# Residual sums of the down projection: VectorE, or ScalarE copies with adding transfers

## The chip, the cores and the metric

The kernel runs on one core of one Trainium2 chip. A core has five engines, each with its own queue of instructions that it works off in order: TensorE (PE in the profile, its weight loads PEld), VectorE (DVE), ScalarE (ACT), GpSimd (POOL) and SyncE (SP). They meet only through semaphores: an instruction that waits holds up everything behind it on its engine. Transfers between the memories run on 16 DMA engines shared by all queues; here SyncE issues the plain loads and GpSimd the adding transfers (`accum_op=ALU.add`), which add what they bring to what the destination holds. Matrix products accumulate in PSUM, whose banks hold 128 x 512 numbers each, and must be read out of it before a bank is used again. All else that is computed on lies in the on-chip memory SBUF.

The metric is the time of one execution in microseconds (us), less is better. Before the change: median 821.08 us of 3 runs (821.05 to 822.15).

## The reference

One decoder layer on 512 tokens of 1024 channels in float32. A mixer (convolution branch, gated linear attention branch, merge, output projection `w_o`) comes first; then the channel mixer, in which the change lies:

```python
h = h + merged @ w_o[l]

u2 = _rmsnorm(h, norm2_g[l])
z = _causal_dwconv(u2 @ w_ffn_up[l], ffn_dw_w[l], ffn_dw_b[l])
h = h + (jax.nn.silu(z[..., :FFN_DIM]) * z[..., FFN_DIM:]) @ w_ffn_down[l]
return _rmsnorm(h, final_g)
```

FFN_DIM is 2816, that is 22 blocks of 128 channels. What concerns us is the last sum: `h` plus the down projection.

## The kernel before

**Products.** Every product in float32 is made of three: each operand is split into a high part rounded to a shorter format (`hi`, cast by ScalarE, L355 or L385) and the rest (`lo`, a subtraction by VectorE, L356 or L390), and `mm3` (L444) multiplies lo by hi, hi by lo and hi by hi into one bank (L448 to L450).

**The residual.** `hres[t, n]` are eight tiles of 128 tokens by 512 channels (t = 0 to 3, n = 0, 1) that hold `h` from the output projection to the end.

**The down projection in three groups.** The 22 channel blocks go in pairs, and the pairs in three groups (`GROUPS`): four pairs, three pairs, four pairs. In each group the up projection of its pairs is computed (`up_plan`), partly together with the first pair of the next group, and then `seven("w_down", ...)` multiplies the group's pairs with `w_ffn_down`. It does so by Strassen's scheme: seven products of block sums in place of eight. The steps have names, in this order: a11; a12 and s1, each in two halves that alternate; n2, s4, n3, a22. Each step makes two products (i = 0 and 1, one for each tile of 128 tokens of one half). Each of the two goes to a bank of its own: a11, n2, n3 and a22 to the pair of banks "x", s1 and s4 to the pair "y", a12 to the pair "z". a11, a12 and s1 start their banks afresh, the others go on adding to what is in theirs. After each product the bank is added to, or subtracted from, one `hres` tile: 14 sums a group (L1419, in `add`), all by VectorE. In the first group a product of one step and one i takes 12 matrix instructions, in the second, with three pairs, 9.

So a bank has to be read before the next step writes it: n3 fills the x banks, its two results are read, and a22 goes on adding to the same banks directly after. Which tiles a step's results go to is written in `into`: a11 and a12 go to `hres[0, 0]` and `hres[1, 0]`; n2 and s4 to `hres[0, 1]` and `hres[1, 1]`; s1 and n3 to `hres[2, 1]` and `hres[3, 1]`; a22 to `hres[2, 0]` and `hres[3, 0]`.

**Weights.** They come in tiles of 128 x 1024 (512 KB; 256 KB where half a tile is needed) into four `raw` buffers or two `kept` buffers, loaded by SyncE (L253, L257, L296). For the scheme, sums of blocks of the weight are needed, too. Three kinds of instruction on GpSimd make them: L300, an adding transfer that sums n3's weight, one for each half; L317, an adding transfer onto `kept`, twice in each group for each half, the second time for a22's weight; and, in the up projection, L327, four additions of 128 x 512 for every pair of tiles (`two_sums`): three after the split of x1's weight and one after the split of x3's. x1, x3, x2 and x4 are the four parts of such a pair's products; x3's weight is what the first two L327 make.

**What sets the order.** Each engine's instructions are put into their order by a planner when the kernel is built; some lines tie it down. In `seven`, the weights that are prepared at a22's call are to be issued behind the last sum of n3 (`freed`). Weights are split two ahead of their use (`LOOK`).

**Small buffers.** `tmp()` gives one of six buffers of 128 x 512 in turn. Until now they serve the up projection: the convolution over tokens (L1500, L1503, L1511) and the pair products (L1181, L1184).

## Time and profile before

| | |
|---|---|
| median of 3 runs | 821.08 us |
| the profiled execution | 820.78 us |
| its span, first to last instruction | 818.9 us |
| TensorE, busy | 810.3 us (99%) |
| VectorE, busy | 715.6 us (87%) |
| ScalarE, busy | 448.9 us (55%) |
| GpSimd, busy | 148.8 us (18%) |
| granted clock of TensorE, mean | 0.999 |
| VectorE's residual sums of 128 x 512, mean of one | 671 ns |

The profile is that of one execution, taken by the hardware profiler. A group line of the page reads: line of the kernel, engine, operation, result <- operands, sizes, count | busy us in total, mean ns of one | idle time of the engine ahead of them, and what ended most of it. A timeline row reads: start, length in us, engine, line, operation; the bracket at the end is the idle time before it and what ended that. A row of a table by stretches gives for each stretch the busy time and count of PE, PEld, DVE, ACT and POOL, then the granted clock, the DMA engines' mean busy share, and GB/s. A row of DMA issues ends with the median time from issue to landing. Times in the timeline run from the span's start; the first group's down projection runs from about 570 to 608 us, the second's from about 671 to 700.

### The profile page before, as it was taken

How to read it: one execution, taken by the hardware profiler on the slowest of the kernel's cores; microseconds unless marked ns; L12 is line 12 of the kernel's file. 1: busy time of each engine (PE TensorE's matmuls, PEld its weight loads, DVE VectorE, ACT ScalarE, POOL GpSimd, SP SyncE). 2: the span in 40 equal slices, each digit the busy share in tenths (PEclk: the TensorE clock that was granted, in tenths of full speed). 3: DMA queues.
4: the chain of work that ended last, by engine and by line, in shares of the span. 5: the costliest groups of instructions: out<-in, count | busy, mean ns of one | idle time of the engine just before them, and what ended most of it. 6: DMA issues, size and time to landing. Idle time of an engine off the chain costs nothing.

```text
span 818.9 us, 11480 instructions
## 1 busy us (share of the span) xinstructions
PE 810.3 (99%) x4287; PEld 700.5 (86%) x4287; DVE 715.6 (87%) x1157; ACT 448.9 (55%) x666; POOL 148.8 (18%) x133
## 2 busy tenths in 40 slices
PE   9999999999999999999999999999999999999996
PEld 7888888888888889999988898898889988899885
DVE  6689999999989699885788889979965999789896
ACT  6643447656663446684444556556435663466554
POOL 2000010001000213633001000230123301622012
PEclk9999999999999999999999999999999999999999
DMA  8355572563532123223657623146642447334662
GB/s 318 104 127 144 148 188 96 130 154 104 120 97 96 49 62 109 88 78 129 206 115 220 187 71 103 52 161 166 134 137 89 144 123 167 104 103 177 158 129 102
DMA packets 30615, 106.25 MB, mean 130 GB/s; under 512 B 3464, under 2 KB 3600, under 8 KB 30560
## 3 DMA queue, kind: packets, MB, share of 16 engines
q1 hardware_dynamic: 24784, 85.34, 30.4%
q0 software_dynamic: 5760, 20.19, 14.4%
q8 instruction: 33, 0.54, 0.3%
q14 instruction: 22, 0.18, 0.1%
q10 hardware_dynamic: 16, 0.00, 0.0%
HBM read 103.42 MB, written 2.10 MB: 129 GB/s over the span
## 4 chain that ended last, share of the span: by engine, by line
PE 98%; DMA 1%; ACT 0%; DVE 0%; POOL 0%; issue 0%; POOLq 0%; SPq 0%; ACTq 0%
PE mm L448 28%; PE mm L449 28%; PE mm L450 28%; PE mm L662 3%; PE ax L450 2%; PE ax L448 2%; PE ax L449 2%; PE ax L1070 1%; PE ax L1072 1%; PE ax L1051 1%; DMA raw<-in_w_v_dram 1%; PE ax L1040 0%; PE ax L529 0%; PE ax L576 0%; PE ax L1085 0%; PE mm L933 0%
## 5 line engine op out<-in xcount | busy, mean ns | idle before, releaser
L448 PE MATMUL mm<-uh,wlo 128*128 128x512 f32 (+1 forms) x672 | 244.4, 364 | 0.0
L449 PE MATMUL mm<-ul,whi 128*128 128x512 f32 (+1 forms) x672 | 242.4, 361 | 0.0
L450 PE MATMUL mm<-uh,whi 128*128 128x512 f32 (+1 forms) x672 | 242.0, 360 | 0.0
L450 PEld LDWEIGHTS mm<-uh,whi 128*128 128x128 f32 x672 | 126.8, 189 | 19.4
L448 PEld LDWEIGHTS mm<-uh,wlo 128*128 128x128 f32 x672 | 127.0, 189 | 18.8
L449 PEld LDWEIGHTS mm<-ul,whi 128*128 128x128 f32 x672 | 127.0, 189 | 18.6
L385 ACT CAST whi<-raw 128x1024 fp32r<-128x1024 f32 x86 | 89.7, 1047 | 54.9 <-PE mm L450 28.2
L356 DVE TENSOR_TENSOR wlo<-raw,whi 128x1024 fp32r<-128x1024 f32 x80 | 93.1, 1171 | 24.4 <-ACT whi L355 20.5
L327 POOL TENSOR_TENSOR raw<-raw,raw 128x512 f32<-128x512 f32 x42 | 67.6, 1610 | 212.8 <-DVE wlo L356 130.7
L390 DVE TENSOR_TENSOR wlo<-raw,whi 128x1024 fp32r<-128x1024 f32 x70 | 92.7, 1327 | 14.1 <-ACT whi L385 14.0
L355 ACT CAST whi<-raw 128x1024 fp32r<-128x1024 f32 x80 | 76.3, 957 | 34.8 <-PE mm L450 27.2
L788 DVE SCALAR_TENSOR_TENSOR c<-h,pp,c 128x255 f32<-128x255 f32 (+14 forms) x120 | 57.5, 479 | 4.0 <-ACT c L784 3.7
L788 DVE SCALAR_TENSOR_TENSOR c<-aside,btmp,c 128x255 f32<-128x255 f32 (+14 forms) x120 | 57.5, 479 | 1.4 <-ACT c L784 1.4
L788 DVE SCALAR_TENSOR_TENSOR aside<-h,pp,aside 128x255 f32<-128x255 f32 (+6 forms) x112 | 53.7, 479 | 0.0
L355 ACT CAST whi<-kept 128x1024 fp32r<-128x1024 f32 (+1 forms) x32 | 31.8, 996 | 31.8 <-DVE kept L310 17.0
L1503 DVE SCALAR_TENSOR_TENSOR tmp<-mm,pp,tmp 128x511 f32<-128x511 f32 (+1 forms) x56 | 41.4, 742 | 4.0 <-ACT tmp L1500 3.9
L356 DVE TENSOR_TENSOR wlo<-kept,whi 128x1024 fp32r<-128x1024 f32 (+1 forms) x32 | 36.8, 1153 | 4.8 <-ACT whi L355 4.7
L1181 ACT COPY tmp<-mm 128x256 f32<-128x256 f32 x48 | 17.7, 368 | 34.4 <-PE mm L450 34.0
L1419 DVE TENSOR_TENSOR hres<-hres,mm 128x512 f32<-128x512 f32 (+1 forms) x49 | 32.3, 671 | 4.7 <-PE mm L450 3.4
L1500 ACT ACTIVATE tmp<-mm,pp 128x512 f32<-128x512 f32 x28 | 21.8, 779 | 19.0 <-PE mm L450 18.9
L387 ACT ACTIVATE wlo<-raw 128x1024 fp32r<-128x1024 f32 x16 | 16.9, 1060 | 22.1 <-PE mm L448 22.1
L1503 DVE SCALAR_TENSOR_TENSOR tmp<-tmp,pp,tmp 128x511 f32<-128x511 f32 (+1 forms) x32 | 27.8, 887 | 0.4
(347 smaller groups left out, 1767.0 us busy)
## 6 DMA issues: line engine op xcount, KB each, us to landing
raw<-in_w_up_dram SPq DMA_DIRECT2D x44, 512.0 KB, 3.5
raw<-in_w_glu_dram SPq DMA_DIRECT2D x16, 512.0 KB, 5.2
raw<-in_w_down_dram SPq DMA_DIRECT2D x15, 512.0 KB, 4.3
kept<-in_w_down_dram POOLq DMA_DIRECT2D x10, 512.0 KB, 5.9
raw<-in_w_v_dram SPq DMA_DIRECT2D x8, 512.0 KB, 5.6
raw<-in_w_qk_dram SPq DMA_DIRECT2D x8, 512.0 KB, 3.4
raw<-in_w_r_dram SPq DMA_DIRECT2D x8, 512.0 KB, 4.6
wlo<-in_w_r_dram POOLq DMA_DIRECT2D x8, 512.0 KB, 8.1
```

The lines of the kernel that those rows point to most:

```text
L327: work = nc.gpsimd.tensor_tensor(out, x, y, ALU.add)
L355: nc.scalar.copy(hi, raw)
L356: two_low[:] = [nc.vector.tensor_tensor(lo, raw, hi.bitcast(F32), ALU.subtract)]
L385: nc.scalar.copy(hi, raw)
L390: pace[0] = nc.vector.tensor_tensor(lo, raw, hi.bitcast(F32), ALU.subtract)
L448: nc.tensor.matmul(acc, ll, rh, start=first, stop=False, **kw)
L449: nc.tensor.matmul(acc, lh, rl, start=False, stop=False, **kw)
L450: nc.tensor.matmul(acc, lh, rh, start=False, stop=last, **kw)
L662: nc.tensor.matmul(acc, act, ready[k // 2][wi][:, j], start=first, stop=last)
L788: nc.vector.scalar_tensor_tensor(out[:, j:], x[:, : half_t - j], w, out[:, j:], ALU.mult, ALU.add)
L1419: done = nc.vector.tensor_tensor(hres[t, n][:, c], hres[t, n][:, c], acc[:, c], op)
L1503: nc.vector.scalar_tensor_tensor(z[:, s:], acc[:, : T - s], w[j], z[:, s:], ALU.mult, ALU.add)
```

## The change

In the first two groups `seven` is called with `aside=True`. There, each of the 14 sums is replaced: ScalarE copies the bank into a `tmp` buffer, with factor 1 or, where the step is subtracted, -1; then GpSimd issues an adding transfer of that buffer onto the `hres` tile, 128 rows of 2 KB from SBUF to SBUF. The instruction that `add` returns, on which `freed` rests, is now ScalarE's copy. The third group, and the output projection, which uses the same function, sum on VectorE as before.

```diff
-    def seven(name, pairs, acts, complete, at=lambda step, i: None, fine=False):
+    def seven(name, pairs, acts, complete, at=lambda step, i: None, fine=False, aside=False):
...
                 def add(n, acc, c=slice(0, T)):
+                    if aside:
+                        term = tmp()
+                        done = nc.scalar.mul(term, acc, 1.0 if op == ALU.add else -1.0)
+                        nc.gpsimd.dma_start(hres[t, n], term, accum_op=ALU.add)
+                        return done
                     done = nc.vector.tensor_tensor(hres[t, n][:, c], hres[t, n][:, c], acc[:, c], op)
                     if whole:
                         complete(t, n, c)
...
         if gi < len(GROUPS) - 1:
-            seven("w_down", pairs, acts, lambda t, n, c: None)
+            seven("w_down", pairs, acts, lambda t, n, c: None, aside=True)
```

In the changed file the copy is L1421 and the transfer L1422. On GpSimd and on ScalarE the new instructions of the second group stand in this order among the others (H is a transfer onto `hres`, C a copy):

```
GpSimd:  L300 (n3, 1st half), H a11, H a11, L300 (n3, 2nd half), H a12, L317 (a22, 1st half),
         H a12, L317 (a22, 2nd half), H s1, H s1, H n2, H n2, H s4, H s4, H n3, H n3,
         L327, L327, L327, H a22, H a22, L327
ScalarE: ... cast s4, cast s4, C n2, cast n3, C n2, cast n3, C s4, cast a22 (1st half),
         C s4, cast a22 (2nd half), C n3, C n3, casts of the up projection (L385, L355),
         C a22, cast x3 (L355), C a22
```

A copy waits until its `tmp` is free, that is until the transfer out of it has landed; an H onto a tile waits on GpSimd until the H before it onto the same tile has landed.

## The prediction

> **What bounds the kernel now.** I read the page first, then who TensorE waits for, then stretches of 5 us around the two groups that change, then single rows there. Lines of the page: busy time of TensorE, the chain that ended last, and four groups (the last numbers are busy us and mean ns of one).

> ```profile
> PE 810.3 (99%) x4287; PEld 700.5 (86%) x4287; DVE 715.6 (87%) x1157; ACT 448.9 (55%) x666; POOL 148.8 (18%) x133
> ...
> PE 98%; DMA 1%; ACT 0%; DVE 0%; POOL 0%; issue 0%; POOLq 0%; SPq 0%; ACTq 0%
> ...
> L356 DVE TENSOR_TENSOR wlo<-raw,whi 128x1024 fp32r<-128x1024 f32 x80 | 93.1, 1171 | 24.4 <-ACT whi L355 20.5
> ...
> L355 ACT CAST whi<-raw 128x1024 fp32r<-128x1024 f32 x80 | 76.3, 957 | 34.8 <-PE mm L450 27.2
> ...
> L1419 DVE TENSOR_TENSOR hres<-hres,mm 128x512 f32<-128x512 f32 (+1 forms) x49 | 32.3, 671 | 4.7 <-PE mm L450 3.4
> L1500 ACT ACTIVATE tmp<-mm,pp 128x512 f32<-128x512 f32 x28 | 21.8, 779 | 19.0 <-PE mm L450 18.9
> ```

> The view of waits, TensorE alone, over the whole run:

> ```profile
> PE mm L568 <- DVE ones L541: 1.1, 1, 1.1
> PE mm L662 <- ACT h L589: 0.8, 1, 0.8
> ```

> Stretches of the first group's products (590 to 595) and the second's (685 to 695); the last two columns are the DMA engines' busy share and GB/s:

> ```profile
> 590.00:595.00 5.00, 5.00 (x24) 4.14 (x23) 4.08 (x7) 2.11 (x2) 0.00 (x0) 1.00 1.04 229
> ...
> 685.00:690.00 5.00, 5.00 (x24) 4.14 (x23) 5.00 (x8) 1.57 (x2) 1.02 (x2) 1.00 0.93 151
> 690.00:695.00 5.00, 5.00 (x24) 4.14 (x23) 4.57 (x8) 1.68 (x2) 0.00 (x0) 1.00 1.01 351
> ```

> TensorE is the bound from end to end. It has two waits of about 1 us, both at the start, and in the stretches it is busy 5.00 of 5.00 at full clock while VectorE is full as well. The one irregularity I found in the changed groups is this, where the second group's n2 begins (TensorE's timeline; products of 512 columns otherwise start 0.23 us apart):

> ```profile
> 683.52 0.61 PE L448 MATMUL mm<-whi,sl 128*128 128x512 f32 x2
> 683.97 0.46 PE L449 MATMUL mm<-wlo,sh 128*128 128x512 f32 x1
> 684.27 0.40 PE L450 MATMUL mm<-whi,sh 128*128 128x512 f32 x1
> ```

> From 683.97 to 684.27 is 0.30, so about 0.07 us is lost there. VectorE relieved by the change can give back 0.07 us, no more. The DMA engines, though, are full (0.93 to 1.04) just where the change adds transfers.

> **What goes, and what comes.** Twenty-eight VectorE sums (14 in each of two groups) go: 28 x 0.67 = 18.8 us of VectorE, off the path, worth 0.07 us. In their place come 28 ScalarE copies of 128x512 out of PSUM, which I price at 0.78 us by the L1500 row (same size, also out of PSUM): 21.8 us on an engine busy 55%. By itself that is hidden: in the second group a bank rests for at least the nine products of the other bank, 9 x 0.23 = 2.0 us. And there come 28 adding transfers of 256 KB on GpSimd's queue. Those I follow, because three kinds of work stand behind them: in GpSimd's own order the weight sums (L317, L300) and the pair sums (L327); in the DMA queue the same weight sums; and in ScalarE's order the next copies, since the six `tmp` buffers come back only when a transfer has landed.

> GpSimd's rows for the second group, then the first, as they are now (start, length):

> ```profile
> 675.35 0.86 POOL L300 DMA_DIRECT2D raw<-in_w_down_dram  x1 [7.27 <-DVE al L1523]
> 683.08 0.87 POOL L300 DMA_DIRECT2D raw<-in_w_down_dram  x1 [6.88 <-DVE hres L1419]
> 684.29 0.85 POOL L317 DMA_DIRECT2D kept<-in_w_down_dram  x1 [0.33 <-issue]
> 685.49 0.88 POOL L317 DMA_DIRECT2D kept<-in_w_down_dram  x1 [0.35 <-DVE wlo L356]
> 696.40 3.54 POOL L327 TENSOR_TENSOR raw<-raw,raw 128x512 f32<-128x512 f32 x2 [10.03 <-DMA raw<-in_w_up_dram]
> ```

> ```profile
> 583.98 0.86 POOL L300 DMA_DIRECT2D raw<-in_w_down_dram  x1 [8.05 <-DVE hres L1419]
> 585.24 0.86 POOL L317 DMA_DIRECT2D kept<-in_w_down_dram  x1 [0.40 <-DVE wlo L356]
> 586.97 0.87 POOL L317 DMA_DIRECT2D kept<-in_w_down_dram  x1 [0.87 <-DVE wlo L356]
> 600.34 3.12 POOL L327 TENSOR_TENSOR raw<-raw,raw 128x512 f32<-128x512 f32 x2 [12.51 <-DVE wlo L356]
> ```

> How long those issues take to land (view of DMA issues in a window around each; last column us to landing). In order: 675.35, 683.08, 684.29, 685.49, then 583.98, 585.24, 586.97:

> ```profile
> raw<-in_w_down_dram POOLq DMA_DIRECT2D x1, 512.0 KB, 5.5
> raw<-in_w_down_dram POOLq DMA_DIRECT2D x1, 256.0 KB, 3.9
> kept<-in_w_down_dram POOLq DMA_DIRECT2D x1, 512.0 KB, 6.2
> kept<-in_w_down_dram POOLq DMA_DIRECT2D x1, 256.0 KB, 7.0
> ...
> raw<-in_w_down_dram POOLq DMA_DIRECT2D x1, 512.0 KB, 5.5
> kept<-in_w_down_dram POOLq DMA_DIRECT2D x1, 512.0 KB, 8.6
> kept<-in_w_down_dram POOLq DMA_DIRECT2D x1, 512.0 KB, 10.6
> ```

> The same view of one adding transfer of 512 KB, 574.9 to 580.5 (q0 is GpSimd's queue; last number its share of the 16 engines), and plain loads of 512 and 256 KB:

> ```profile
> q0 software_dynamic: 144, 0.52, 59.1%
> ...
> raw<-in_w_down_dram SPq DMA_DIRECT2D x1, 512.0 KB, 3.6
> ...
> raw<-in_w_down_dram SPq DMA_DIRECT2D x1, 256.0 KB, 2.6
> ```

> An adding transfer of 512 KB costs 0.591 x 5.6 = 3.3 us of all engines. 512 and 256 KB differ by 5.5 - 3.9 = 1.6, so 256 KB costs 1.6. And q0 works its transfers off one behind the other: 583.98 + 5.5 = 589.5, 585.24 + 8.6 = 593.8, 586.97 + 10.6 = 597.6, steps of 4.3 and 3.8. Beyond 3.3 each, that is 1.5 us lost to the weight loads that share the engines; in the second group 687.0 + 3.3 + 1.6 = 691.9 against 692.5, so 0.6. I take 1.5 for both groups, since the second's queue will now last as long as its loads do.

> No row of before adds from SBUF to SBUF. From below it is bounded by a plain load: 2.6 us to landing, 1.3 under the 3.9 of the adding one, so 0.3 of service; from above by the 3.3 of the double size. I take c = 1.6, the row with the same rows, bytes, queue and addition; only the source differs.

> **Second group, step by step.** These are the rows of TensorE that set the dates, in order: a22 begins in the first group, x3 of the next pair's up projection, then the same two in the second group.

> ```profile
> 602.80 0.39 PE L448 MATMUL mm<-whi,al 128*128 128x512 f32 x1
> ...
> 616.58 0.28 PE L448 MATMUL mm<-xq,wlo 128*128 128x256 f32 x1
> ...
> 695.86 0.39 PE L448 MATMUL mm<-whi,al 128*128 128x512 f32 x1
> ...
> 708.27 0.28 PE L448 MATMUL mm<-xq,wlo 128*128 128x256 f32 x1
> ```

> In the changed program a22's first product writes the bank that n3 filled, so the copy of n3's first sum must be done by 695.86 and begin by 695.1. That copy is the eleventh of the group, and its `tmp` was the fifth's: it waits until s1's first sum has landed. On GpSimd's order that transfer stands behind these: a11's two sums (behind the L300 of 675.35: 675.35 + 5.5 + 2c = 684.1), L300 (issued about 1.3 earlier, since the two sums that stood ahead of its buffer's split, 2 x 0.67, are gone: 681.8, + 3.9 = 685.7; by the queue 684.1 + 1.6, the same), a12's first sum (c), L317 of 512 KB (3.3), a12's second sum (c), L317 of 256 KB (1.6), itself (c). Sum: 685.7 + 3 x 1.6 + 3.3 + 1.6 = 695.4, with 1.5 for the loads 696.9. The copy ends and TensorE starts a22 at 697.7: a stall of 1.8 us. In ScalarE's order the cast of the second L317's weight stands directly ahead of that copy, so it too arrives late (about 695.3 against 692.55 now):

> ```profile
> 692.55 0.62 ACT L355 CAST whi<-kept 128x512 fp32r<-128x512 f32 x1 [0.20 <-DMA kept<-in_w_down_dram]
> ```

> What is late next: GpSimd. s4's two transfers add to the same `hres` tiles as n2's and wait on GpSimd for those to land; n3's two and then L327 stand behind. s1's second, n2's first and second land by 696.9 + 3 x 1.6 = 701.7; then three issues at 1.2 us (683.08 to 684.29): L327 starts 705.3 instead of 696.40, and ends 708.8 (3.54); cast and split (L355, L356; 2.2 with their hand-overs 2.3) make 711.1. x3 needs it at 708.27 + 1.8 = 710.1: another 1.0 us.

> [...]

> **First group.** L300 1.3 earlier, 582.7, landed 588.2; L317 3.3, a12 twice c, L317 3.3, s1's first c: 588.2 + 6.6 + 4.8 + 1.5 = 601.1. The copy must begin by 602.80 - 0.78 = 602.0: 0.9 to spare. L327: 601.1 + 4.8 + 3 x 1.2 = 609.5, + 3.1 + 2.3 = 614.9 against 616.58: 1.7 to spare. No stall. It is the fourth pair's products (12 instead of 9 for each bank) that hide it; were the queue 0.9 us slower, every further us would show.

> **Also moved, at no cost.** SyncE loads the next pair's weight when the last L327 of this one frees its buffer (first row: now, 704.53 + 2.21 = 706.7); its split must stand before that pair's x1 (second row).

> ```profile
> 704.53 2.21 POOL L327 TENSOR_TENSOR raw<-raw,raw 128x512 f32<-128x512 f32 x1 [2.37 <-DVE wlo L356]
> ...
> 720.95 0.28 PE L448 MATMUL mm<-uh,wlo 128*128 128x256 f32 x1
> ```

> The third L327 (2.3) ends at 711.1, a22's two issues at 713.5, the last L327 at about 716; a load lands 3.6 later (a plain 512 KB in the same view), cast and split make 722 against 720.95 + 2.8 = 723.8. Cover 1.8 us; in the first group it is larger. The other loads follow VectorE's splits, which come earlier, and the third group keeps its VectorE sums.

> **Sum.** 1.8 + 1.0 - 0.07 = 2.7 us. The profiled run took 820.78 (span 818.9 and 1.9 around it), so 823.5; the median, 821.08, lies 0.3 above it: **823.8 us**.

> **Rivals.** *The transfers are cheap* (chance 0.22). The 1.8 is 685.7 + 3c + 4.9 + 1.5 - 695.1, nothing at c = 1.0; at 1.4 both stalls together are 1.6 us. At c of 1.0 or less all is hidden: 821.0 to 821.1. For it: a source in SBUF; against it: the additions in the rows, 3.3 against plain loads. [...]

> *The transfers are dearer* (0.20). At c = 2.2 the sums give 4.8 + 2.8 in the second group (a11's two now hold up L300 by 1.2) and 1.2 + 1.1 in the first: 9.8, so 830.9. At the upper bound 3.3 they give 16.4 and some 11: 848. For it: two reads of the same memory, which no row has; against it: 3.9 is a measured row of the same 128 rows of 2 KB.

> *VectorE's relief pays* (0.04): faster. Splits come earlier and TensorE runs closer. It decides only if the copies never wait (c up to 1.0), and then it has the 0.07 us of 683.97 to win: 821.0. To count it would need 1.6 us of pauses that the waits don't show.

> **Numbers.** 0.2%, 1.6 us, is about what a measurement here can tell. Forecast 0.54 (822.7 to 827), dearer 0.20, cheap 0.22, relief 0.04. Slower by over 0.2%: 0.54 + 0.20 = 0.74; within: 0.22; faster: 0.04. The range goes from hidden to a little past c = 2.2: 820.9 to 831.0.

> **What would show it.** Right: TensorE waits for ScalarE's copy (L1421) at n3's bank in the second group, about 2 us, none or little in the first; copies whose idle time there ends on the landing of a `hres` transfer; L327 about 9 us later; landings of `hres` transfers growing from 4 to 9 us. Wrong: landings of 3 us or less; a stall already in the first group; or TensorE waiting for anything on VectorE.

## The result, and the profile after

The changed kernel takes 833.62 us (median of 4 runs, 832.89 to 835.03) against 821.07 for the kernel before: a ratio of 1.0151, with a 95% interval of 1.0139 to 1.0164. Slower was right. The size was not: 2.7 us were forecast, and 12.5 came, past the end of the range. The profiled execution took 832.89, with a span of 831.0, 12.1 longer than before.

The page of the changed kernel: busy time, the chain that ended last, the group of the new transfers; below them the one new entry in the list of TensorE's waits (total, times, longest):

```profile
PE 813.4 (98%) x4287; PEld 702.0 (84%) x4287; DVE 699.9 (84%) x1129; ACT 463.0 (56%) x694; POOL 171.2 (21%) x161
...
PE 89%; DMA 3%; issue 3%; DVE 3%; POOL 1%; ACT 1%; POOLq 0%; SPq 0%; ACTq 0%; DVEq 0%
...
L1422 POOL DMA_DIRECT2D hres<-tmp x28 | 25.4, 935 | 23.8 <-issue 14.3
```

```profile
PE mm L448 <- ACT tmp L1421: 9.0, 2, 6.9
```

VectorE is relieved by 15.7 us (715.6 to 699.9), and none of it shortens the time. The chain is on TensorE for 89% of the span instead of 98%. Both new waits are where the prediction put its one: a22's first product waits for the copy of n3's first sum. TensorE's timeline around them:

```profile
602.71 0.39 PE L450 MATMUL mm<-whi,yh 128*128 128x512 f32 x1
605.19 0.50 PE L448 MATMUL mm<-whi,al 128*128 128x512 f32 x1 [2.08 <-ACT tmp L1421]
...
698.09 0.39 PE L450 MATMUL mm<-whi,yh 128*128 128x512 f32 x1
705.39 0.80 PE L448 MATMUL mm<-whi,al 128*128 128x512 f32 x1 [6.91 <-ACT tmp L1421]
705.99 0.63 PE L449 MATMUL mm<-wlo,ah 128*128 128x512 f32 x1
...
710.25 0.61 PE L450 MATMUL mm<-whi,ah 128*128 128x512 f32 x1
710.68 0.42 PE L448 MATMUL mm<-whi,al 128*128 128x512 f32 x1
```

Products normally start 0.23 us apart. So the first pause is 605.19 - 602.71 - 0.23 = 2.25, the second 705.39 - 698.09 - 0.23 = 7.07. Behind the first one TensorE is 2.46 late (698.09 + 0.23 against 695.86). Behind the second the products themselves are slow: the 12 from 705.39 to 710.68 take 5.29 instead of 2.72. The stretches say why (columns as before: PE, PEld, DVE, ACT, POOL, then the granted clock, the DMA share, GB/s):

```profile
695.00:700.00 5.00, 3.48 (x16) 2.55 (x14) 0.00 (x0) 0.91 (x2) 1.17 (x2) 1.00 1.03 245
700.00:705.00 5.00, 0.00 (x0) 0.00 (x0) 1.92 (x2) 1.95 (x4) 2.25 (x4) 0.55 1.10 231
705.00:710.00 5.00, 4.61 (x11) 3.65 (x12) 2.36 (x2) 3.17 (x5) 1.69 (x2) 0.50 0.82 143
710.00:715.00 5.00, 5.00 (x23) 4.09 (x22) 0.00 (x0) 0.24 (x1) 4.54 (x5) 0.93 1.07 234
```

The granted clock fell to 0.50 during the second pause and stayed there after it, which took 5.29 - 2.72 = 2.57. That makes the account: 2.46 + 7.07 + 2.57 = 12.1, the whole difference of the spans.

**Where the pauses come from.** GpSimd's rows that decide, first group then second: L300 of n3's second half, then the issue of s1's first transfer, whose landing frees the `tmp` that n3's copy needs.

```profile
585.78 0.87 POOL L300 DMA_DIRECT2D raw<-in_w_down_dram  x1 [7.65 <-DMA raw<-in_w_down_dram]
...
599.21 0.84 POOL L1422 DMA_DIRECT2D hres<-tmp  x1 [1.72 <-issue]
...
687.50 0.86 POOL L300 DMA_DIRECT2D raw<-in_w_down_dram  x1 [7.07 <-DMA raw<-in_w_down_dram]
...
699.64 0.87 POOL L1422 DMA_DIRECT2D hres<-tmp  x1 [3.83 <-issue]
```

Both L300 waited for the landing of the plain load onto which they add. SyncE issued those loads at 578.69 and 681.13, about 1.1 earlier than before (the second reckoned without the 2.46), near the 1.3 that was forecast for the L300 behind them. The view of DMA issues gives their landings (first two lines), then those of the two L300 and of s1's two transfers, in order:

```profile
raw<-in_w_down_dram SPq DMA_DIRECT2D x1, 512.0 KB, 6.4
...
raw<-in_w_down_dram SPq DMA_DIRECT2D x1, 256.0 KB, 5.6
...
raw<-in_w_down_dram POOLq DMA_DIRECT2D x1, 512.0 KB, 5.5
...
raw<-in_w_down_dram POOLq DMA_DIRECT2D x1, 256.0 KB, 3.8
...
hres<-tmp POOLq DMA_DIRECT2D x1, 256.0 KB, 5.2
...
hres<-tmp POOLq DMA_DIRECT2D x1, 256.0 KB, 5.0
```

The loads took 6.4 and 5.6 us instead of 3.6 and 2.6. So L300 landed at 591.28 and 691.30, where 588.2 and 685.7 had been forecast: 3.1 late, and again 3.1 late once the 2.46 is taken off. From there to the landing of s1's first transfer (604.41, 704.64) it is 13.1 and 13.3 us, where the prediction had 12.9 and 11.2.

By ScalarE's rows, more `tmp` buffers would not have saved the second pause. In ScalarE's order the cast of a22's second half stands ahead of n3's copy, and it waited for its own weight sum (L317):

```profile
703.40 0.62 ACT L355 CAST whi<-kept 128x512 fp32r<-128x512 f32 x1 [0.78 <-DMA kept<-in_w_down_dram]
704.74 0.60 ACT L1421 ACTIVATE tmp<-mm 128x512 f32<-128x512 f32 x1 [0.72 <-DMA hres<-tmp]
```

With a free buffer the copy could have begun about 0.7 us earlier (0.2 in the first group, by the same two rows there). This is an estimate from these rows; no run had more buffers.

The theory to test, then: first, a11's transfers slow the plain load, and L300 starts late; second, in the second group the queue behind L300 is 2.1 us longer than forecast, through the other plain loads; third, the clock takes the rest. Rivals: the copies themselves; a limit on how many transfers GpSimd keeps under way; transfers that are dearer than 1.6 us.

### The profile page after: what moved, and what is told of

It reads as the page before. It is cut to its first block, busy times and chain, and to the rows that moved or that the text cites. A ratio compares the mean times of both kernels' runs of the same rounds, so it can differ in the third digit from the quotient of the medians.

```text
span 831.0 us, 11559 instructions
## 1 busy us (share of the span) xinstructions
PE 813.4 (98%) x4287; PEld 702.0 (84%) x4287; DVE 699.9 (84%) x1129; ACT 463.0 (56%) x694; POOL 171.2 (21%) x161
## 4 chain that ended last, share of the span: by engine, by line
PE 89%; DMA 3%; issue 3%; DVE 3%; POOL 1%; ACT 1%; POOLq 0%; SPq 0%; ACTq 0%; DVEq 0%
PE mm L448 25%; PE mm L449 25%; PE mm L450 25%; PE mm L662 3%; PE ax L450 2%; PE ax L449 2%; PE ax L448 2%; DMA raw<-in_w_down_dram 1%; DMA hres<-tmp 1%; DVE tmp L1508 1%; PE ax L1070 1%; DVE wlo L356 1%; PE ax L1072 1%; PE ax L1051 1%; DMA raw<-in_w_v_dram 1%
## 5 line engine op out<-in xcount | busy, mean ns | idle before, releaser
L448 PE MATMUL mm<-uh,wlo 128*128 128x512 f32 (+1 forms) x672 | 244.4, 364 | 0.0
L449 PE MATMUL mm<-ul,whi 128*128 128x512 f32 (+1 forms) x672 | 242.3, 361 | 0.0
L450 PE MATMUL mm<-uh,whi 128*128 128x512 f32 (+1 forms) x672 | 242.0, 360 | 0.0
L450 PEld LDWEIGHTS mm<-uh,whi 128*128 128x128 f32 x672 | 126.8, 189 | 19.5
L448 PEld LDWEIGHTS mm<-uh,wlo 128*128 128x128 f32 x672 | 127.0, 189 | 18.9
L449 PEld LDWEIGHTS mm<-ul,whi 128*128 128x128 f32 x672 | 127.0, 189 | 18.5
L356 DVE TENSOR_TENSOR wlo<-raw,whi 128x1024 fp32r<-128x1024 f32 x80 | 93.8, 1177 | 43.1 <-ACT whi L355 39.5
L327 POOL TENSOR_TENSOR raw<-raw,raw 128x512 f32<-128x512 f32 x42 | 68.2, 1623 | 175.5 <-DVE wlo L356 95.8
L355 ACT CAST whi<-raw 128x1024 fp32r<-128x1024 f32 x80 | 76.4, 957 | 33.3 <-PE mm L450 19.5
L356 DVE TENSOR_TENSOR wlo<-kept,whi 128x1024 fp32r<-128x1024 f32 (+1 forms) x32 | 36.7, 1153 | 21.5 <-ACT whi L355 21.4
L355 ACT CAST whi<-kept 128x1024 fp32r<-128x1024 f32 (+1 forms) x32 | 31.7, 994 | 26.8 <-DVE kept L310 12.3
L1505 ACT ACTIVATE tmp<-mm,pp 128x512 f32<-128x512 f32 x28 | 21.8, 777 | 17.4 <-PE mm L450 17.2
L1422 POOL DMA_DIRECT2D hres<-tmp x28 | 25.4, 935 | 23.8 <-issue 14.3
## 6 DMA issues: line engine op xcount, KB each, us to landing
raw<-in_w_up_dram SPq DMA_DIRECT2D x44, 512.0 KB, 4.0
raw<-in_w_glu_dram SPq DMA_DIRECT2D x16, 512.0 KB, 4.9
raw<-in_w_down_dram SPq DMA_DIRECT2D x15, 512.0 KB, 5.2
hres<-tmp POOLq DMA_DIRECT2D x28, 256.0 KB, 4.8
kept<-in_w_down_dram POOLq DMA_DIRECT2D x10, 512.0 KB, 6.4
raw<-in_w_v_dram SPq DMA_DIRECT2D x8, 512.0 KB, 5.6
raw<-in_w_qk_dram SPq DMA_DIRECT2D x8, 512.0 KB, 3.4
raw<-in_w_r_dram SPq DMA_DIRECT2D x8, 512.0 KB, 4.5
```

Of the source, the lines that this page charges most:

```text
L327: work = nc.gpsimd.tensor_tensor(out, x, y, ALU.add)
L355: nc.scalar.copy(hi, raw)
L356: two_low[:] = [nc.vector.tensor_tensor(lo, raw, hi.bitcast(F32), ALU.subtract)]
L448: nc.tensor.matmul(acc, ll, rh, start=first, stop=False, **kw)
L449: nc.tensor.matmul(acc, lh, rl, start=False, stop=False, **kw)
L450: nc.tensor.matmul(acc, lh, rh, start=False, stop=last, **kw)
```

## The experiments

Times of the experiments are compared with runs of the kernel before on the same chip (medians 821.1 to 821.6 us); the ratios are to those.

### Copies without transfers

```diff
                         done = nc.scalar.mul(term, acc, 1.0 if op == ALU.add else -1.0)
-                        nc.gpsimd.dma_start(hres[t, n], term, accum_op=ALU.add)
                         return done
```

> The 28 adding transfers are left out, the 28 ScalarE copies stay, so the first two groups' results never reach the residual. Theory (the loss comes from the transfers alone): no wait of TensorE for a copy, full clock throughout, span 818.9, time 820.8 to 821.1. Rival (the copies themselves, at 0.60 us each on an engine that also casts the weights, cost something): TensorE waits for ScalarE at n3's bank or for a cast, 822 or more. VectorE's relief could show here, too: below 820.4 if it is worth more than the 0.07 us that the prediction gave it.

820.91 us, ratio 0.9991 (0.9982 to 1.0000). TensorE waits for no copy, and the clock stays full in both groups. A copy took 0.60 us (median 599 ns). The whole loss comes from the transfers, and VectorE's relief without them is worth at most 0.2%.

This kernel also shows what the earlier load does by itself. TensorE runs 0.70 late in this execution, in both groups (s1's first product at 579.02 against 578.32, and 678.78 against 678.08). With that taken off, the loads are issued 1.2 us earlier in both groups. In the second group the load takes 2.5 us and L300 starts 1.3 earlier (682.50, that is 681.80), as was forecast. In the first group the load takes 4.5 us, and L300 starts only 0.2 earlier (584.48, that is 583.78). So about 1.1 of the 3.1 us by which the first group's L300 is late in the changed kernel are there without any transfer; why that load takes 4.5 is not shown. The rest, and the whole delay of the second group, need the transfers.

### The transfers overwrite

```diff
-                        nc.gpsimd.dma_start(hres[t, n], term, accum_op=ALU.add)
+                        nc.gpsimd.dma_start(hres[t, n], term)
```

> The 28 transfers overwrite the residual tile instead of adding to it, so the residual sums are wrong; size, queue, waits and order are the same. If the adding is what costs (the destination is read as well), 256 KB takes well under 1.3 us alone and 14 of them a group leave the queue 5 us or more earlier: waits of TensorE of 2 us or less in all, 821 to 824. If a transfer from SBUF to SBUF costs the same without the adding, the waits stay at 2.1 and 6.9 us, 833.

825.85 us, ratio 1.0049 (1.0035 to 1.0063): a third of the loss stays, somewhat more than the 821 to 824 expected for costly adding. The two loads ahead of L300 take 5.4 and 3.9 us, between those without transfers and those beside adding ones. GpSimd's queue on the pages of the kernel without transfers, this one, and the changed kernel (packets, MB, share of 16 engines):

```profile
q0 software_dynamic: 5760, 20.19, 13.9%
```

```profile
q0 software_dynamic: 8000, 27.53, 16.4%
```

```profile
q0 software_dynamic: 9792, 27.53, 19.1%
```

With the spans 819.5, 824.7 and 831.0 that is 113.9, 135.3 and 158.7 us of all engines. Per transfer: adding (158.7 - 113.9) / 28 = 1.60 us, overwriting (135.3 - 113.9) / 28 = 0.76. So c = 1.6 was right, and the adding is half of it. (The kernel before has 14.4% of 818.9, that is 117.9; with that as the start, adding comes out at 1.46. The runs with 16 and 24 adding transfers, 17.1% of 818.8 and 18.4% of 827.2, lie at 1.63 and 1.60 above the 113.9, so 1.6 holds better.) The landings say the same (all 28, overwriting, then adding):

```profile
DMA to landing us min/median/max: 2.3/5.4/11.7
```

```profile
DMA to landing us min/median/max: 3.2/4.8/11.9
```

The shortest overwriting one, 2.3 us, is near the 2.6 of the plain load of 256 KB in the kernel before; the shortest adding one is 0.9 above it. The cheap rival needed 1.0 us of all engines or less for each transfer. Without the adding, 0.76, that was so; with it, 1.60, it was not, and the rival fell.

### More room for descriptors

While three adding transfers are under way, GpSimd issues no fourth in the changed kernel: of L1422's idle time 14.3 us ended on nothing that the profile shows, each time about 0.3 us after a landing (L317 of 586.40 landed 9.9 later, at 596.3; the next issue is at 596.62).

```diff
-    nc = _bacc.Bacc("TRN2", target_bir_lowering=False, num_devices=1, dynamic_dma_scratch_size=1024)
+    nc = _bacc.Bacc("TRN2", target_bir_lowering=False, num_devices=1, dynamic_dma_scratch_size=2048)
```

> The room for GpSimd's transfer descriptors is doubled from 1024 to 2048 bytes; nothing else changes. Theory (the engines are full, 1.03 to 1.10 in the stretches, so it does not matter that GpSimd has no more than three adding transfers under way): the idle time of GpSimd before an issue, 14.3 us in the group of L1422, shrinks, landings get longer by as much, s1's first sum still lands 13 us after L300, the waits stay at 2.1 and 6.9 us within 0.5, 833 to 834. Rival (the limit of three leaves gaps in the queue that cost the time): s1's first sum lands 2 us or more earlier, the second wait falls below 5 us, 831 or less.

834.31 us, ratio 1.0147 (1.0132 to 1.0162), as the changed kernel. GpSimd now issues eight without a gap:

```profile
585.32 0.86 POOL L300 DMA_DIRECT2D raw<-in_w_down_dram  x1 [7.31 <-DMA raw<-in_w_down_dram]
586.03 1.04 POOL L317 DMA_DIRECT2D kept<-in_w_down_dram  x1
586.63 2.21 POOL L1422 DMA_DIRECT2D hres<-tmp  x2
587.80 1.95 POOL L317 DMA_DIRECT2D kept<-in_w_down_dram  x1
588.35 4.01 POOL L1422 DMA_DIRECT2D hres<-tmp  x3
```

The landings grow by what the issues gained (median 6.7 us instead of 4.8); the pauses are 3.1 and 6.6 us instead of 2.2 and 7.1. The limit exists and costs nothing here: with the DMA share at 1.03 to 1.10 in most of the stretches above, the engines are full.

### a11's sums back on VectorE, and a11's alone

```diff
-                    if aside:
+                    if aside and step != "a11":
```

> a11's two sums of each group go back to VectorE, the other 24 stay as ScalarE copies and adding transfers. Theory (a11's transfers fill the DMA engines while the plain load of n3's second half runs, so the L300 that adds onto it starts 3.1 and 3.5 us late): the load takes about 3.6 us again, L300 starts near 584.0 and 683.1 as in the kernel before and lands near 589.5 and 687.0; with the 13.1 and 13.3 us from there to the landing of s1's first sum, TensorE waits about 0.6 us in the first group and about 2.6 us in the second, and the clock stays at 1.0: 821.1 + 3.2 = 824.3. Rival (it is the length of the queue behind L300, not its start): two transfers of 1.6 us less bring 3 us at most, the second wait stays above 4 us, the clock falls, 829 or more.

829.92 us, ratio 1.0094 (1.0077 to 1.0111). The rows are those of the theory: the loads take 3.3 and 2.5 us, L300 starts at 583.82 and 683.11, and the first group's pause is gone. The loads' landings, first group and second:

```profile
raw<-in_w_down_dram SPq DMA_DIRECT2D x1, 512.0 KB, 3.3
...
raw<-in_w_down_dram SPq DMA_DIRECT2D x1, 256.0 KB, 2.5
```

The time, though, is that of the rival (829 or more, the second wait above 4 us, the clock fallen), so the time alone would not decide; the start of L300 does. The number was wrong by an oversight in the expectation. The 2.6 us of pause took L300's 4.3 us off the changed kernel's 6.9, but in that kernel TensorE comes to the second group 2.46 later, and here it does not. With that it is 5.1, and 5.4 was measured, at 0.50 of the clock afterwards. Nor are the loads issued earlier here (579.89 and 679.90, as before), since VectorE does a11's sums again; so this run takes away both the transfers beside the load and its earlier issue, and it needs the copies alone, above, and the next run to tell these apart.

The reverse:

```diff
-                    if aside:
+                    if aside and step == "a11":
```

> Only a11's two sums of each of the two groups are copies and transfers (4 of 28). Theory (a11's transfers by themselves make the plain load of n3's second half, and so L300, late): the load takes 6 us instead of 3.6 and 2.6, L300 starts near 585.7 and 685.2 instead of 584.0 and 683.1, although nothing else of the change is there; behind it the queue has only the weight sums, and no copy waits: no pause, 821.0 to 821.3. Rival (L300 is late because of what stands ahead of it on GpSimd or because of a buffer): L300 stays within 0.5 us of 584.0 and 683.1.

822.34 us, ratio 1.0014 (1.0005 to 1.0023). With two transfers a group and nothing else of the change, the loads take 7.0 and 5.0 us:

```profile
raw<-in_w_down_dram SPq DMA_DIRECT2D x1, 512.0 KB, 7.0
...
raw<-in_w_down_dram SPq DMA_DIRECT2D x1, 256.0 KB, 5.0
```

L300 starts at 586.52 and 684.86: the first later than expected, the second in between. In this run, the one before and the copies alone, as in the kernel before and the changed one, L300 begins 0.6 to 0.8 us after its load has landed, whatever its bracket names. The expected "no pause" did not come: there are two small ones, at a22 in both groups (0.3 and 0.7 us by the starts of TensorE's products). By the rows they come from the weight sums behind L300. In the second group the cast of a22's second half waits until 695.05 for its weight sum, VectorE's split of it follows at 695.70, and n3's sums stand behind that split at 696.31; the first group shows the same order (split 601.40, sum 602.54, a22 at 603.37). So a late L300 costs about a microsecond even where nothing waits for a copy.

The second load is issued at 679.26 here and at 679.27 in the kernel with the copies alone, where it took 2.5 us and not 5.0. Around that load the two runs differ in a11's transfers alone, so the theory's first part is shown.

### Smaller loads beside the queue

```diff
+                    few = slice(0, 32 if p in (10, 14) else D)
                     for raw, m in zip(pair_raws[name, p], (p, q)):
-                        nc.sync.dma_start(raw, a[name][m])
+                        nc.sync.dma_start(raw[:, few], a[name][m][:, few])
+                        if p in (10, 14):
+                            nc.vector.memset(raw[:, 32:], 0.0)
...
             raw = raw_tile()
-            nc.sync.dma_start(raw, a[name][j])
+            few = slice(0, 32 if name == "w_up" and j in (9, 13) else D)
+            nc.sync.dma_start(raw[:, few], a[name][j][:, few])
+            if few.stop == 32:
+                nc.vector.memset(raw[:, 32:], 0.0)
```

> The three plain loads of the next up projection that fall among the transfers of each of the two groups (L257 and the pair of L253) bring 32 of their 1024 columns; VectorE fills the rest with zeros, so those weights are wrong. The transfers and their order are the same. Theory (these loads cost the queue 1.7 us in the first group and 3.6 in the second, where the prediction took 1.5 for each): from the landing of L300 to that of s1's first sum 11.4 and 9.7 us instead of 13.1 and 13.3; pauses 0.5 and 3.5 us, and up to 2 us to the clock: 825 to 827. Rival (the transfers alone are slower than 1.6 us each while several are under way): 13 us stay, pauses as in the changed kernel, 832 to 834.

825.32 us, ratio 1.0047 (1.0032 to 1.0062). L300 lands at 591.3 and 689.0, s1's first transfer at 602.95 and 698.5: 11.7 and 9.5 us, so the three loads of each group, but for the little that they still bring, cost the queue 1.5 us in the first group and 3.8 in the second. What is left, 11.7 and 9.5, is what the transfers come to at 1.6 and 3.3 us each (11.4 and 9.7), so they are not slower than that. The prediction took 1.5 for both. The pauses are 0.50 and 2.53 (3.5 were expected for the second), and with the second, short as it is, the clock was at 0.50 for 3.4 us.

### One group at a time

```diff
-            seven("w_down", pairs, acts, lambda t, n, c: None, aside=True)
+            seven("w_down", pairs, acts, lambda t, n, c: None, aside=gi == 0)
```

> Copies and transfers in the first group alone; the second sums on VectorE. Theory (the two groups add up): TensorE pauses once, about 2.2 us at n3's bank in the first group, and loses 0.2 more; clock 1.0; 821.1 + 2.4 = 823.5. Rival (a transfer left over at the group's end delays the next up projection as well): a further wait behind the first group, 825 or more.

For the second group alone, `gi == 1`:

> Copies and transfers in the second group alone. Theory: the same late L300 (2.4 us earlier than in the changed kernel, since the first group no longer shifts everything) and the same pause of 7.1 us, and the clock at 0.50 for the 12 products behind it, so 821.1 + 7.1 + 2.6 = 830.8; how much the clock takes can differ by a microsecond or so. With the first group alone (823.5) the two differences add up to that of the change, 12.1 to 12.5. Rival (the second group is hit because the first one leaves GpSimd and the loads late): the pause is below 5 us, 828 or less.

The second group alone: 829.69 us, ratio 1.0103 (1.0088 to 1.0118), a pause of 6.92 and the clock at 0.50, as expected; the first group is not its cause. The first group alone: 826.7 us, ratio 1.0071 (1.0054 to 1.0088). Its profiled execution is as expected (823.29, one pause of 2.36, full clock), but the other three took 825.9 to 828.0. By the medians the two differences come to 8.5 and 5.5 us, together 14.0 and not the 12.1 to 12.5 expected; by the profiled spans they are 10.1 and 2.7. Hence the first group alone once more:

> The kernel with the first group alone once more, since three of its four runs took 825.9 to 828.0 and the profiled one 823.3. [...] Rival (the pause itself gets longer): 4 us or more of pause at full clock. [...]

The profiled execution took 827.25 (the second of the two 825.78). TensorE's row:

```profile
606.40 0.79 PE L448 MATMUL mm<-whi,al 128*128 128x512 f32 x1 [3.07 <-ACT tmp L1421]
```

The pause did get longer, but not to 4 us: it is 3.24, 0.9 longer, and L300 started 0.9 later (586.60 against 585.66; 0.2 of it the whole execution is late), again behind the plain load, which took 7.0 us instead of 6.3. Nor was the clock full: it fell to 0.50 during this pause, at 605.49, and stayed there until 612.32, which by half of the 5.92 us from 606.40 on is 2.96 us more. 3.24 + 2.96 = 6.2, of a difference of the spans of 6.5.

### Without a11 and a12, and the last four steps alone

```diff
-                    if aside:
+                    if aside and step not in ("a11", "a12"):
```

> a11's and a12's sums go back to VectorE in both groups; s1, n2, s4, n3 and a22 stay as copies and transfers (20 of 28). Theory: L300 as in the kernel before (584.0, 683.1; landed 589.5, 687.0). First group: 589.5 + 3.3 + 3.3 + 1.6 + 1.7 for the loads = 599.4, before 602.0, no pause. Second: 687.0 + 3.3 + 1.6 + 1.6 + 3.6 = 697.1 for s1's first sum, the copy ends 697.9, against 695.9: a pause of 2.0 us, which like the 2.25 us of the changed kernel's first group leaves the clock at 1.0. 823.1. Rival (limited by the number under way, not by the work of the queue): pause above 4 us and the clock at 0.50, 826 or more; or, if a12's transfers were the larger part, no pause and 821.1.

825.65 us, ratio 1.0056 (1.0041 to 1.0071). No pause in the first group, one of 2.28 in the second, near the 2.0 expected, but by another way: n3's copy stood in ScalarE's order behind the cast of a22's second half, whose weight sum (L317) had not landed.

```profile
697.72 0.62 ACT L355 CAST whi<-kept 128x512 fp32r<-128x512 f32 x1 [2.76 <-DMA kept<-in_w_down_dram]
698.24 0.59 ACT L1421 ACTIVATE tmp<-mm 128x512 f32<-128x512 f32 x1
```

And the clock did not stay at 1.0, which took 1.7 us more.

```diff
-                    if aside:
+                    if aside and step in ("n2", "s4", "n3", "a22"):
```

> Copies and transfers for n2, s4, n3 and a22 only (16 of 28); a11, a12 and s1 on VectorE. Theory: n3's copies no longer take the buffers of s1's transfers, and the weight sums stand ahead of all transfers on GpSimd, so TensorE never waits and L327 of the second group starts near 698 instead of 696.4, with some 6 us of room before x3: 821.0 to 821.3, within 0.2% of the kernel before. Rival (any transfer beside the weight sums costs): the casts of a22's weights come late, TensorE waits for one of them or for x3's split, 822.8 or more.

821.29 us in 11 runs, ratio 1.0000 (0.9991 to 1.0009). Sixteen of the 28 sums can be moved at no cost: their transfers stand behind the weight sums on GpSimd, and n3's copies wait for no buffer of an earlier one. The run does not tell which of the two matters more. L327 starts at 701.73, later than the 698 expected, and nothing waits for it. Nothing is gained by them, either.

### What the clock took

The clock's edges can be read from stretches of 0.1 us (the third number from the end). The changed kernel, second group, fall and rise:

```profile
700.40:700.50 0.10, 0.00 (x0) 0.00 (x0) 0.00 (x0) 0.08 (x1) 0.10 (x1) 0.85 1.09 348
...
710.70:710.80 0.10, 0.10 (x2) 0.10 (x1) 0.00 (x0) 0.00 (x0) 0.10 (x1) 0.94 1.00 102
```

The kernel without a11 and a12:

```profile
699.80:699.90 0.10, 0.10 (x2) 0.09 (x1) 0.00 (x0) 0.00 (x0) 0.00 (x0) 0.58 1.38 266
...
703.20:703.30 0.10, 0.10 (x1) 0.10 (x1) 0.10 (x1) 0.10 (x1) 0.00 (x0) 0.85 0.00 0
```

A mean of 0.85 over 0.1 us is a fall to 0.50 at 700.47; in the same way the rise is at 710.71: 10.24 us. The other gives 699.82 to 703.23: 3.41. All stretches at 0.50 that these runs show in the two groups are 3.41, 6.83 or 10.24 us long. What that makes of the time, in us (at 0.50 products start 0.43 us apart instead of 0.23, nearly twice, so the loss is about half of what lies between the pause's end, or the fall where it comes later, and the rise):

| kernel | pauses | at 0.50 | lost to the clock | sum | span less 818.9 |
|---|---|---|---|---|---|
| the change | 2.25; 7.07 | 10.24 | 2.6 | 11.9 | 12.1 |
| more descriptors | 3.08; 6.64 | 3.4; 6.8 | 1.7 + 2.2 | 13.6 | 13.6 |
| a11 on VectorE | 5.44 | 6.8 | 2.9 | 8.3 | 8.3 |
| second group | 6.92 | 10.2 | 3.0 | 9.9 | 10.1 |
| first group, again | 3.24 | 6.8 | 3.0 | 6.2 | 6.5 |
| overwriting | 0.73; 2.90 | 3.4 | 1.7 | 5.3 | 5.8 |
| small loads | 0.50; 2.53 | 3.4 | 1.7 | 4.7 | 5.1 |
| from s1 on | 2.28 | 3.4 | 1.7 | 4.0 | 5.0 |
| first group | 2.36 | none | none | 2.4 | 2.7 |
| a11's alone | 0.32; 0.69 | none | none | 1.0 | 1.4 |

The pauses and the clock explain nearly all of every one. What is left is within 0.2 us of what each execution was already late when s1's first product began, 0.1 to 0.4 us and in the kernel from s1 on 0.8 (579.09 against 578.32); there no sum of that kernel had been moved yet, so it is not the change. With a pause of 2.36 us the clock stayed full; with one of 2.28 (until 698.88, in the kernel from s1 on) it fell to 0.50 at 699.82, 0.94 us after the pause's end. So in these runs the length of a pause alone does not tell whether the clock falls; what else does is not shown.

## Why the prediction was wrong

By its own steps:

- **TensorE is the bound, and VectorE's relief can win 0.07 us.** Right: 0.9991 with the copies alone, 1.0000 with 16 sums moved. (VectorE was not full in all the stretches shown, but busy 4.08 to 5.00 of 5 us; nothing rests on it.)
- **28 copies at 0.78, hidden.** Hidden; each took 0.60.
- **c = 1.6, 3.3 for 512 KB, one behind the other.** Right: 1.60 by the queue's share, and twice the descriptors changed nothing.
- **"L300 issued about 1.3 earlier": 582.7 and 681.8.** This is the step that failed. The prediction moved L300 with the two VectorE sums, as its bracket `<-DVE hres L1419` suggests, and has no term for the plain load onto which L300 adds. In those rows, too, L300 began 0.6 and 0.7 us after that load had landed (579.76 + 3.6 = 583.4 and 679.77 + 2.6 = 682.4). In the changed kernel the load was issued about 1.1 earlier, but a11's two transfers ran beside it. The prediction counted these in GpSimd's queue, where they did not hold L300 up, and not against the load. It took 6.4 and 5.6 us instead of 3.6 and 2.6, and L300 started 3.1 and 3.2 us later than forecast. Of the first group's 3.1, the copies alone already show 1.1.
- **First group: no stall, 0.9 to spare, and past that every further us shows.** The balance was right: 3.1 less 0.9 is 2.2, and 2.25 came. The conclusion fell with the step above.
- **1.5 us for the loads, in both groups.** 1.5 in the first, 3.8 in the second: a term mis-sized by 2.3. The prediction took the second group's from the first's row, since the queue there would now last as long as the loads do; its own row of before gave 0.6.
- **Second group: a stall of 1.8 at n3's bank.** The right place, `tmp` and transfer. 1.8 plus 3.1 for L300's landing and 2.1 for the longer queue (13.3 against 11.2) is 7.0: 7.07 came.
- **Another 1.0 at x3.** Did not show. L327 began at 712.55, later still than the forecast 705.3, but the pause in front of it had put off x3 as well. The wait of s4 on n2 that this step counts with came: n2's transfers (issued at 703.63 and 704.97, 3.5 and 4.7 us to landing) landed at 707.1 and 709.7, and s4's were issued at 707.84 and 710.38, each 0.7 us later.
- **The cover of the next pair's load.** No wait of TensorE shows there.
- **Not in the prediction:** the clock, 2.6 us. The forecast pause was 1.8 us; with one of 2.28 the clock fell to 0.50. No run shows one between 0.73 and 2.25.

From 2.7 forecast: less 1.0 at x3, plus 2.5 in the first group, 3.1 + 2.1 in the second, and 2.6 from the clock, is 12.0, against 12.1 in the spans. That the time was longer at all was forecast by the right wait at the right bank; most of the size came from what the prediction left out. Of its rivals, "dearer" came near with 830.9 and a stall in both groups, but for a reason that did not hold: the transfers cost what was forecast; the loads beside them cost more. Of its signs, a stall in the first group was named as one that would show it wrong, and it did; the landings grew past the 9 us named, to 11.9.

## What to carry to other kernels

A new transfer is to be priced twice: by its own service, and by what it does to every load that runs beside it and that something waits for. The first was forecast rightly here; the second was missed, 2 to 3 us on a load that stood ahead of the whole queue. Put new transfers behind the transfers that have a due time: the 16 that stood behind the weight sums were free, and the four of a11 alone cost about a microsecond. And where a pause of TensorE as long as those here (2.25 us and more) is forecast, add a clock term. Here it was nothing twice (after 2.25 and 2.36 us) and otherwise 1.7 to 3.0 us.
